# First-MLP weights of a two-layer encoder trunk: rounded by a casting DMA, with remainders formed by an adding DMA, in place of a plain load, a cast and a subtraction

## The chip, the cores and the metric

The kernel runs on one core of one Trainium2 chip. The metric is device time in microseconds: 1135.37 us as the median of 3 runs (1135.32 to 1135.9). An engine is named as the profile names it: PE (TensorE, matmuls), PEld (its weight loads), DVE (VectorE), ACT (ScalarE), POOL (GpSimd), SP (SyncE, whose queue issues all DMAs of the kernel before).

## The reference

The input x has 512 tokens of 1024 features. Two layers, each a token mixer and an MLP:

```python
for i in range(DEPTH):                      # DEPTH = 2: latent attention, then mLSTM
    hn = rms_norm(x, norm_mix[i])
    y = mla_mixer(hn, ...) if i == 0 else mlstm_mixer(hn, ...)
    x = x + y
    x = x + sqrelu_mlp(rms_norm(x, norm_ffn[i]), ffn_w1[i], ffn_w2[i])

def sqrelu_mlp(h, w1, w2):                  # w1: 1024 x 4096, w2: 4096 x 1024
    return jnp.square(jax.nn.relu(h @ w1)) @ w2
```

All in float32. The change touches the loading of w1 alone.

## The kernel before

**Products of three.** Every large product is made of operands that are split in two: `hi`, the value rounded to the short float type that PE takes (fp32r), and `lo`, the remainder, rounded likewise. `mm3` (L175) multiplies hi by hi, hi by lo and lo by hi into one accumulator. For weights the split is `split_w` (L155): the raw float32 tile `wr` arrives by DMA (`load_raw`, L150, on SP's queue), ACT casts it to `wh` (hi), DVE subtracts `wh` from `wr` and writes `wl` (lo). Each of the tags `wr`, `wh`, `wl` has three buffers that rotate.

**The stages.** `mla`, `ffn` of layer 0 (about 240 to 581 us), `mlstm`, `ffn` of layer 1 (about 810 to 1134 us). The MLP's hidden size of 4096 is worked in 8 chunks of 512, each as four blocks of 128 hidden features. A block ("F", `f_mm`, L749) is 24 matmuls: 8 slices of the model dimension, three products each, 512 tokens wide. Its third matmul is the first to read `wl`. After it, ACT applies relu and the square (`f_post`, L755); after every second block (odd numbers) POOL forms four sums over the squares (the tile `z`, four instructions in a row, 128x256 each), which ACT and DVE then split into `hh` and `hl`.

The second product uses a scheme with 7 products ("P", `s_mm`, L806) in place of 8 for each chunk but the last, each of 12 matmuls. Its weights come by SP as float32 tiles `tw` and are combined by POOL into t1, t2, t3, t4 (`s_sum`, L792, 128x1024 each) before they are split like the others.

**The order of the work.** It is written out: `units` (L867 to L874) lists blocks and products in PE's order. It begins with blocks 0 to 4; then, in a chunk, with the blocks named after their place:

```
P0 Fa P1 P2 Fb P3 P4 Fc P5 Fd P6
```

Fa of the first chunk is block 5, Fb block 6, and so on to block 28; the last chunk has only blocks 29, 30, 31, after its first, second and fourth product. When PE is at one unit, `ahead` (L877) loads the block that is four units further on (`f_load`, L743) and splits the weights of the unit that is two units further on (`f_split`, L746, or `s_split`, L803). Blocks 0 and 1 are loaded and split earlier, in `out_proj` (L712), and are not touched by the change, which leaves 30 blocks in each MLP.

Inside `ffn` all engines keep the order of the program for what is issued through `ipe`, `idve`, `iact` and `ipool` (L83, L731); so each engine works down one queue. `f_post` puts its four z sums on POOL's queue at once and the splits of z one and two units later (`later`, L783).

Of the kernel before, what the change touches and what calls it, by code (L numbers as in the profile page):

```python
# [16 lines left out]
F32 = mybir.dt.float32  # L17
F32R = mybir.dt.float32r
AF = mybir.ActivationFunctionType
# [3 lines left out]
P = 128  # L23
T = 512
NB = T // P
D = 1024
# [16 lines left out]
WMAX = 1280  # L43
# [18 lines left out]
def trunk(ctx: ExitStack, tc, a, yT, dbg=None):  # L62
    nc = tc.nc
    mult, add, sub, amax, amin, apow = ALU.mult, ALU.add, ALU.subtract, ALU.max, ALU.min, ALU.pow
    cp = ctx.enter_context(tc.tile_pool(name="cp", bufs=1))
    wp = ctx.enter_context(tc.tile_pool(name="wp", bufs=3))
# [16 lines left out]
    ipe, idve, iact, ipool = (InOrder(nc.tensor), InOrder(nc.vector), InOrder(nc.scalar, False), InOrder(nc.gpsimd, False))  # L83
    uid = [0]

    def nm(s):
        uid[0] += 1
        return f"{s}_{uid[0]}"
# [61 lines left out]
    def load_raw(src, n):  # L150
        raw = wp.tile([P, WMAX], F32, tag="wr", name=nm("wr"))
        nc.sync.dma_start(raw[:, :n], src)
        return raw

    def split_w(raw, n, act=nc.scalar, dve=nc.vector, dve2=None, m=0, to=None):  # L155
        if to is not None:
            hi, lo = to[0], to[1]
        else:
            hi = wp.tile([P, WMAX], F32R, tag="wh", name=nm("wh"))
            lo = wp.tile([P, WMAX], F32R, tag="wl", name=nm("wl"))  # L160
        if act in (nc.scalar, iact):
            act.copy(hi[:, :n], raw[:, :n])  # L162
        else:
            act.tensor_copy(hi[:, :n], raw[:, :n])
        if dve is dve2 or not dve2:
            dve.tensor_sub(lo[:, :n], raw[:, :n], hi[:, :n].bitcast(F32))  # L166
        else:
            dve.tensor_sub(lo[:, :m], raw[:, :m], hi[:, :m].bitcast(F32))
            dve2.tensor_sub(lo[:, m:n], raw[:, m:n], hi[:, m:n].bitcast(F32))
        return hi, lo  # L170
# [555 lines left out]
    def ffn(fp, layer, last):  # L726
# [12 lines left out]
        zs, hs, raws, ws, tw, bank, later, s_now = {}, {}, {}, {}, {}, {}, [], [1]  # L739
# [1 line left out]


        def f_load(i):  # L743
            raws[i] = load_raw(a["w1"][layer, i // 4 * 4 + (0, 2, 1, 3)[i % 4]], D)

        def f_split(i):  # L746
            ws["F", i] = split_w(raws.pop(i), D, iact, idve)

        def f_mm(ps, i, c=slice(0, T)):  # L749
            hi, lo = ws["F", i]  # L750
# [126 lines left out]
        def ahead(s_):  # L877

            if s_ + 4 < len(units) and units[s_ + 4][0] == "F":
                f_load(units[s_ + 4][1])  # L880
            if s_ + 2 < len(units):
                u = units[s_ + 2]
                if u[0] == "F":
                    f_split(u[1])
                else:
                    s_split(u[1], u[2])
                    if u[2] == 0:
                        s_sum(u[1], "t2")
                    elif u[2] == 1:
                        s_sum(u[1], "t4")  # L890


        ws["F", 0], ws["F", 1] = norm.first
        f_load(2)
        ps = [ps_mm(), ps_mm()]
        f_mm(ps[0], 0, HALVES[0])
        for do in norm.tail:
            do()
        f_mm(ps[1], 1, HALVES[0])
        f_load(3)  # L900
        f_split(2)
        f_mm(ps[0], 0, HALVES[1])
        f_post(ps[0], 0)
        f_mm(ps[1], 1, HALVES[1])
        f_load(4)
        f_split(3)
        f_post(ps[1], 1)
        s_load(0, ("b11", "b12"))
# [371 lines left out]
```

## Time and profile before

| | |
|---|---|
| median of 3 runs | 1135.37 us (1135.32 to 1135.9) |
| profiled execution, its own time | 1136.02 us |
| span of the profiled execution | 1134.0 us |
| granted TensorE clock, mean over the span | 0.998 of full speed |
| PE busy | 1111.6 us (98%) |
| DVE busy | 823.3 us (73%) |
| ACT busy | 557.9 us (49%) |
| POOL busy | 451.4 us (40%) |
| DMA | 104.27 MB, 30.1% of 16 engines' span, all on SP's queue but instructions |

How to read it. All times are from one profiled execution and count from its span's start; 2.0 us of its time lie around the span. A timeline's row gives the start, the duration, the engine, the line, the operation with output and inputs, how many instructions were merged (their time is then that of the row), and, in brackets, how long the engine idled before and whom it waited for. Matmuls overlap: on PE the distance between two starts (0.23 us for 512 columns) is what a matmul costs, and its duration is longer. Many instructions carry line 80, which is the helper that records them; they are told apart by their tiles. DMA-issuing instructions are not counted as busy.

### The profile page before, as it was taken

The numbers are of one execution on the slowest core, as the hardware profiler recorded it, in microseconds if no ns is written. First come the engines' busy times: TensorE is split into PE (matmuls) and PEld (weight loads), VectorE is DVE, ScalarE is ACT, GpSimd is POOL, SyncE is SP. The second block draws the span as 40 slices with busy tenths as digits, with TensorE's granted clock in tenths as the row PEclk, the third lists the DMA queues.
The fourth block names the chain that finished last, engine by engine and source line by source line (L and its number), as shares of the span: only waits on it lengthen the run. The fifth ranks groups of instructions, "written<-read, shape, count | busy, mean of one in ns | idle before, by whom it ended". The sixth has DMA issues, their size and how long they took to land.

```text
span 1134.0 us, 15668 instructions
## 1 busy us (share of the span) xinstructions
PE 1111.6 (98%) x5802; PEld 949.0 (84%) x5802; DVE 823.3 (73%) x1286; ACT 557.9 (49%) x985; POOL 451.4 (40%) x454
## 2 busy tenths in 40 slices
PE   7899999999999999999999999999999999999998
PEld 7889988888888888888898898888888888888886
DVE  7689997456798798788756565554578779779863
ACT  4468876336544444534545344332655444444441
POOL 6667785207356347335010011000537437436500
PEclk9999999999999999999999999999999999999999
DMA  6301021433432432343203223232343343333112
GB/s 202 117 25 47 20 76 38 132 98 124 128 99 74 127 112 84 102 123 89 85 21 100 87 59 91 81 90 86 136 113 91 93 130 93 93 112 111 57 56 75
DMA packets 32428, 104.27 MB, mean 92 GB/s; under 512 B 3424, under 2 KB 6752, under 8 KB 32352
## 3 DMA queue, kind: packets, MB, share of 16 engines
q1 hardware_dynamic: 32352, 103.27, 30.1%
q8 instruction: 46, 0.75, 0.3%
q14 instruction: 30, 0.25, 0.1%
HBM read 101.16 MB, written 2.10 MB: 91 GB/s over the span
## 4 chain that ended last, share of the span: by engine, by line
PE 93%; DVE 3%; POOL 2%; ACT 1%; issue 1%; DMA 0%; SPq 0%; ACTq 0%; POOLq 0%
PE mm L80 39%; PE tp L80 38%; PE mm L178 4%; PE mm L177 4%; PE mm L176 4%; PE po L80 3%; PE tp L178 1%; PE tp L177 1%; PE tp L176 1%; DVE wl L80 1%; ACT t L80 1%; DVE x L80 1%; POOL x L80 0%; DMA x<-in_xT 0%; POOL scr L80 0%
## 5 line engine op out<-in xcount | busy, mean ns | idle before, releaser
L80 PE MATMUL mm<-xg,wh 128*128 128x512 f32 (+1 forms) x1088 | 319.1, 377 | 0.0
L80 POOL TENSOR_TENSOR z<-z 128x256 f32<-128x256 f32 x112 | 129.5, 1175 | 320.2 <-ACT z L80 318.0
L80 PEld LDWEIGHTS mm<-xg,wh 128*128 128x128 f32 x1088 | 200.2, 188 | 37.4
L80 DVE TENSOR_TENSOR wl<-tw,wh 128x1024 fp32r<-128x1024 f32 x100 | 174.5, 1745 | 74.9 <-ACT wh L80 74.9
L80 PE MATMUL mm<-xg,wl 128*128 128x512 f32 (+1 forms) x544 | 206.3, 379 | 0.0
L80 POOL TENSOR_TENSOR tw<-tw,tw 128x1024 f32<-128x1024 f32 x56 | 159.8, 2862 | 34.6 <-issue 29.2
L80 DVE SCALAR_TENSOR_TENSOR x<-tp,r,x 128x512 f32<-128x512 f32 (+1 forms) x215 | 149.8, 733 | 14.2 <-PE tp L80 14.1
L80 PE MATMUL tp<-wh,hl 128*128 128x512 f32 x408 | 159.0, 390 | 0.9 <-DVE hl L80 0.9
L80 DVE TENSOR_TENSOR wl<-wr,wh 128x1024 fp32r<-128x1024 f32 (+1 forms) x72 | 119.6, 1661 | 55.4 <-ACT wh L80 55.4
L80 PE MATMUL tp<-wh,hh 128*128 128x512 f32 x408 | 159.1, 390 | 0.0
L80 PE MATMUL tp<-wl,hh 128*128 128x512 f32 x408 | 158.7, 389 | 0.0
L80 ACT ACTIVATE t<-mm 128x512 f32<-128x512 f32 (+3 forms) x97 | 54.3, 560 | 204.1 <-PE mm L80 195.0
L80 PEld LDWEIGHTS mm<-xg,wl 128*128 128x128 f32 x544 | 102.3, 188 | 22.9 <-DVE wl L80 4.5
L80 ACT CAST wh<-tw 128x1024 fp32r<-128x1024 f32 x100 | 104.7, 1047 | 34.1 <-PE tp L80 26.2
L80 ACT CAST wh<-wr 128x1024 fp32r<-128x1024 f32 (+1 forms) x74 | 78.9, 1067 | 32.1 <-PE tp L80 27.7
L166 DVE TENSOR_TENSOR wl<-wr,wh 128x1024 fp32r<-128x1024 f32 (+2 forms) x43 | 51.2, 1194 | 55.8 <-ACT wh L162 55.6
L80 PEld LDWEIGHTS tp<-wh,hl 128*128 128x128 f32 x408 | 76.6, 188 | 17.7 <-DVE hl L80 1.7
L80 PEld LDWEIGHTS tp<-wh,hh 128*128 128x128 f32 x408 | 76.6, 188 | 16.5 <-ACT zw L80 0.8
L80 PEld LDWEIGHTS tp<-wl,hh 128*128 128x128 f32 x408 | 76.6, 188 | 15.8
L80 ACT CAST hh<-z 128x1024 fp32r<-128x1024 f32 (+1 forms) x60 | 56.9, 949 | 53.0 <-POOL z L80 53.0
L80 DVE TENSOR_TENSOR hl<-z,hh 128x1024 fp32r<-128x1024 f32 (+1 forms) x60 | 80.7, 1345 | 0.0
L162 ACT CAST wh<-wr 128x1024 fp32r<-128x1024 f32 (+2 forms) x43 | 42.8, 995 | 66.7 <-PE mm L177 31.6
(281 smaller groups left out, 2063.7 us busy)
## 6 DMA issues: line engine op xcount, KB each, us to landing
wr<-in_w SPq DMA_DIRECT2D x64, 512.0 KB, 3.6
tw<-in_w SPq DMA_DIRECT2D x64, 512.0 KB, 3.6
wr<-in_w_qkv SPq DMA_DIRECT2D x8, 640.0 KB, 4.1
wr<-in_w_oa SPq DMA_DIRECT2D x8, 512.0 KB, 3.7
wr<-in_w_mo SPq DMA_DIRECT2D x8, 512.0 KB, 3.5
wr<-in_w_ob SPq DMA_DIRECT2D x8, 512.0 KB, 3.6
wr<-in_w_v SPq DMA_DIRECT2D x6, 512.0 KB, 3.9
wr<-in_w_z SPq DMA_DIRECT2D x8, 336.0 KB, 4.9
```

What stands on the lines that cost most here:

```text
L80: return lambda *args, **kw: tc.keep_in_program_order(f(*args, **kw)) if self.on else f(*args, **kw)
L162: act.copy(hi[:, :n], raw[:, :n])
L166: dve.tensor_sub(lo[:, :n], raw[:, :n], hi[:, :n].bitcast(F32))
L176: pe.matmul(out, lhsT=lh, rhs=rh, start=start, stop=False)
L177: pe.matmul(out, lhsT=lh, rhs=rl, start=False, stop=False)
L178: pe.matmul(out, lhsT=ll, rhs=rh, start=False, stop=stop)
```

## The change

`f_load` no longer loads float32 through SP. It takes a buffer of the tag `wr` as fp32r tile (`wfh`) and lets POOL issue a DMA from the float32 weights into it, which is to round on the way. `f_split` no longer casts on ACT and subtracts on DVE: ACT writes the negated rounded weights into `wl`, and a second DMA, issued by POOL, reads the same weights from HBM once more and adds them to `wl`. PE multiplies the same `hi` and `lo` in the same order. Blocks 0 and 1 of each MLP, and all other weights, stay as they were.

```diff
         def f_load(i):
-            raws[i] = load_raw(a["w1"][layer, i // 4 * 4 + (0, 2, 1, 3)[i % 4]], D)
+
+            raws[i] = wp.tile([P, WMAX], F32R, tag="wr", name=nm("wfh"))
+            ipool.dma_start(raws[i][:, :D], f_src(i))
+
+        def f_src(i):
+            return a["w1"][layer, i // 4 * 4 + (0, 2, 1, 3)[i % 4]]
 
         def f_split(i):
-            ws["F", i] = split_w(raws.pop(i), D, iact, idve)
+
+            hi = raws.pop(i)
+            lo = wp.tile([P, WMAX], F32R, tag="wl", name=nm("wl"))
+            iact.activation(lo[:, :D], hi[:, :D].bitcast(F32), AF.Copy, scale=-1.0)
+            ipool.dma_start(lo[:, :D], f_src(i), accum_op=add)
+            ws["F", i] = hi, lo
```

On POOL's queue, one chunk in the middle of the first MLP, from the z sums after a block Fc to the z sums after the next block Fa. `z` are the sums over squares, `tw` the weight sums t1, t2, t3, t4 in this order. Before:

```order
L80 TENSOR_TENSOR z_4153<-z_4153 128x256 x4
L80 TENSOR_TENSOR tw_4259<-tw_4122,tw_4120 128x1024
L80 TENSOR_TENSOR tw_4120<-tw_4197,tw_4259 128x1024
L80 TENSOR_TENSOR tw_4122<-tw_4197,tw_4122 128x1024
L80 TENSOR_TENSOR tw_4259<-tw_4195,tw_4120 128x1024
L80 TENSOR_TENSOR z_4293<-z_4293 128x256 x4
```

And now, with the DMAs behind the second z sums as well (`wfh` is a load, `wl` an adding DMA):

```order
L80 TENSOR_TENSOR z_4144<-z_4144 128x256 x4
L80 DMA wfh_4238<-in_w 128x1024
L80 TENSOR_TENSOR tw_4248<-tw_4113,tw_4111 128x1024
L80 TENSOR_TENSOR tw_4111<-tw_4187,tw_4248 128x1024
L80 DMA wl_4298<-in_w 128x1024
L80 TENSOR_TENSOR tw_4113<-tw_4187,tw_4113 128x1024
L80 DMA wfh_4318<-in_w 128x1024
L80 TENSOR_TENSOR tw_4248<-tw_4185,tw_4111 128x1024
L80 TENSOR_TENSOR z_4282<-z_4282 128x256 x4
L80 DMA wl_4379<-in_w 128x1024
L80 DMA wfh_4398<-in_w 128x1024
L80 DMA wfh_4457<-in_w 128x1024
```

The adding DMA of the next Fa (`wl_4298`) stands behind t1 and t2, that of Fb (`wl_4379`) behind the four z sums of Fa; the adding DMAs of Fc and Fd follow the two loads that end the piece.

On ACT's queue, the same place, from the relu of a block Fd to the split for P1. Before:

```order
L80 ACTIVATE t_4294<-mm_4261 128x512
L80 ACTIVATE z_4293<-t_4294 128x2x256
L80 CAST wh_4309<-wr_4249 128x1024
L80 CAST wh_4332<-tw_4259 128x1024
L80 CAST wh_4364<-tw_4120 128x1024
```

And now:

```order
L80 ACTIVATE t_4283<-mm_4250 128x512
L80 ACTIVATE z_4282<-t_4283 128x2x256
L80 ACTIVATE wl_4298<-wfh_4238 128x1024
L80 CAST wh_4320<-tw_4248 128x1024
L80 CAST wh_4352<-tw_4111 128x1024
```

The cast of the block's weights has become the negated copy, in the same place.

On POOL's queue, the start of the first MLP. Before:

```order
L80 TENSOR_TENSOR z_3529<-z_3529 128x256 x4
L80 TENSOR_TENSOR tw_3576<-tw_3574,tw_3572 128x1024
L80 TENSOR_TENSOR tw_3574<-tw_3580,tw_3574 128x1024
L80 TENSOR_TENSOR tw_3572<-tw_3580,tw_3576 128x1024
L80 TENSOR_TENSOR z_3616<-z_3616 128x256 x4
```

And now (`wfh_3411`, `wfh_3499`, `wfh_3556`, `wfh_3606` load blocks 2, 3, 4, 5; `wl_3501`, `wl_3558`, `wl_3608` add for blocks 2, 3, 4):

```order
L80 DMA wfh_3411<-in_w 128x1024
L80 DMA wfh_3499<-in_w 128x1024
L80 DMA wl_3501<-in_w 128x1024
L80 DMA wfh_3556<-in_w 128x1024
L80 DMA wl_3558<-in_w 128x1024
L80 TENSOR_TENSOR z_3528<-z_3528 128x256 x4
L80 TENSOR_TENSOR tw_3574<-tw_3572,tw_3570 128x1024
L80 TENSOR_TENSOR tw_3572<-tw_3578,tw_3572 128x1024
L80 DMA wfh_3606<-in_w 128x1024
L80 DMA wl_3608<-in_w 128x1024
L80 TENSOR_TENSOR tw_3570<-tw_3578,tw_3574 128x1024
L80 TENSOR_TENSOR z_3613<-z_3613 128x256 x4
```

The adding DMA of block 4 stands behind two weight sums and the load of block 5. PE's queue is the same in both kernels; DVE's has lost 60 subtractions, SP's 60 loads, and nothing else on them has moved.

## Rows read from the trace of the kernel before

**Rows 1.** The page: PE's busy time, and the chain that ended last by engine.

```profile
PE 1111.6 (98%) x5802; PEld 949.0 (84%) x5802; DVE 823.3 (73%) x1286; ACT 557.9 (49%) x985; POOL 451.4 (40%) x454
...
PE 93%; DVE 3%; POOL 2%; ACT 1%; issue 1%; DMA 0%; SPq 0%; ACTq 0%; POOLq 0%
```

**Rows 2.** PE's waits in the two MLPs: us in total, times, longest us.

```profile
PE tp L80 <- DVE hl L80: 0.4, 1, 0.4
PE mm L80 <- DVE xg L80: 0.3, 1, 0.3
...
PE mm L80 <- DVE x L80: 0.9, 1, 0.9
PE tp L80 <- DVE hl L80: 0.5, 1, 0.5
```

**Rows 3.** Timeline of PE, a chunk of the first MLP: beginnings of Fb, Fc, Fd, Fa.

```profile
370.59 0.62 PE L80 MATMUL mm<-xg,wh 128*128 128x512 f32 x2
371.04 0.39 PE L80 MATMUL mm<-xg,wl 128*128 128x512 f32 x1
...
381.92 0.39 PE L80 MATMUL mm<-xg,wl 128*128 128x512 f32 x1
...
390.08 0.39 PE L80 MATMUL mm<-xg,wl 128*128 128x512 f32 x1
...
400.51 0.61 PE L80 MATMUL mm<-xg,wh 128*128 128x512 f32 x2
```

**Rows 4.** Timeline of ACT, same chunk: casts for Fb, Fc, Fd and Fa.

```profile
366.52 1.03 ACT L80 CAST wh<-wr 128x1024 fp32r<-128x1024 f32 x1
...
377.39 1.03 ACT L80 CAST wh<-wr 128x1024 fp32r<-128x1024 f32 x1
...
381.67 1.05 ACT L80 CAST wh<-wr 128x1024 fp32r<-128x1024 f32 x1 [1.66 <-PE tp L80]
...
396.43 1.04 ACT L80 CAST wh<-wr 128x1024 fp32r<-128x1024 f32 x1
```

**Rows 5.** Groups by form, DVE, 240 to 581 us: busy, mean ns, idle before.

```profile
L80 DVE TENSOR_TENSOR wl<-wr,wh 128x1024 fp32r<-128x1024 f32 x31 | 54.6, 1760 | 27.5 <-ACT wh L80 27.5
L80 DVE TENSOR_TENSOR hl<-z,hh 128x768 fp32r<-128x768 f32 x14 | 20.9, 1491 | 0.0
```

**Rows 6.** The page's DMA issues: KB each, us from issue to landing.

```profile
wr<-in_w SPq DMA_DIRECT2D x64, 512.0 KB, 3.6
```

**Rows 7.** Timeline of SP's queue: one such load being issued.

```profile
401.05 0.33 SPq L152 DMA_DIRECT2D wr<-in_w  x1
```

**Rows 8.** Groups by form, whole span: POOL's instruction on 128x4 elements.

```profile
L80 POOL TENSOR_TENSOR scr<-sm,nhalf 128x4 f32<-128x4 f32 x32 | 34.0, 1064 | 2.4
```

**Rows 9.** Busy time by stretch (length, engines, granted clock, DMA share, GB/s).

```profile
8.00:9.00 1.00, 1.00 (x5) 0.98 (x6) 0.65 (x3) 0.58 (x1) 0.00 (x0) 1.00 1.09 393
```

**Rows 10.** Timeline of POOL, same chunk: z sums of Fa, then t1, then t2, t3.

```profile
366.69 4.83 POOL L80 TENSOR_TENSOR z<-z 128x256 f32<-128x256 f32 x4 [0.84 <-ACT z L80]
...
393.05 2.41 POOL L80 TENSOR_TENSOR tw<-tw,tw 128x1024 f32<-128x1024 f32 x1
396.68 6.60 POOL L80 TENSOR_TENSOR tw<-tw,tw 128x1024 f32<-128x1024 f32 x2 [1.22 <-issue]
```

**Rows 11.** Timeline of POOL, start of the first MLP: first two weight sums.

```profile
263.93 4.87 POOL L80 TENSOR_TENSOR tw<-tw,tw 128x1024 f32<-128x1024 f32 x2
```

**Rows 12.** Timeline of PE, start of the first MLP: block 4's third matmul.

```profile
269.13 0.39 PE L80 MATMUL mm<-xg,wl 128*128 128x512 f32 x1
```

**Rows 13.** Busy time by stretch in the attention stage, columns as in Rows 9.

```profile
62.00:64.00 2.00, 0.54 (x5) 0.30 (x3) 1.16 (x5) 1.17 (x4) 1.92 (x3) 1.00 0.00 0
64.00:66.00 2.00, 1.32 (x6) 0.97 (x7) 2.00 (x10) 0.25 (x1) 2.00 (x3) 0.96 0.19 34
66.00:68.00 2.00, 2.00 (x9) 1.81 (x9) 1.56 (x8) 0.57 (x2) 1.63 (x3) 0.50 0.79 289
68.00:70.00 2.00, 1.99 (x13) 1.75 (x11) 1.66 (x6) 1.05 (x5) 1.58 (x3) 0.68 0.03 13
```

## The prediction

> **What bounds the kernel now.** I read the page first, then TensorE's waits, then one chunk engine by engine in the timeline.
>
> [rows 1] PE is busy for 98% of the span and makes 93% of the chain that ended last; DVE makes 3%. [rows 2] In the two stages that the change touches (240 to 581 us, and 810 to 1134 us) PE waited 0.4, 0.3, 0.9 and 0.5 us, 2.1 us in all, each for a DVE result of another kind (hl, xg, x), none for a first-MLP remainder. So there is next to nothing to win there: what the change takes off DVE, PE doesn't wait for. What can move the time is a remainder (`wl`) that comes later than PE's third matmul of the block, the first one that reads it.
>
> How near that is shows in one chunk. [rows 3] Block Fb begins at 370.59 and reads its remainder at 371.04, 0.45 us later; Fc reads its at 381.92, Fd at 390.08; the next chunk's Fa begins at 400.51, so it reads at 400.96. [rows 4] ACT makes these four rounded copies at 366.52, 377.39, 381.67 and 396.43, and DVE has some 2 us left for the subtraction behind the first two.
>
> **The change, part by part.**
>
> *DVE.* 60 subtractions leave it: 30 blocks in each of the two MLPs. [rows 5] They cost 1.76 us each there, some 106 us in all. No wait of PE hangs on them [rows 2], so I put the gain at nothing.
>
> *ACT.* 60 casts become 60 scaled copies of the same tile in the same place of ACT's order. I price them as the casts, 1.03 to 1.05 us [rows 4], and the difference at nothing.
>
> *SP.* 60 loads leave its queue, which then holds only second-MLP loads. PE waits for none of these [rows 2]: nothing.
>
> *POOL.* 120 DMAs come in, and they stand in POOL's queue between its sums. The load of a block is issued four units before its use and can be late without harm. The adding DMA is the critical one: it can start only when ACT has the negated copy **and** POOL is past what stands ahead of it. Before, ACT and DVE alone made the remainder.
>
> Price of one adding DMA, D, from POOL being free to the tile having landed. No row shows a DMA issued by POOL or one that adds. [rows 6] A plain 512 KB load lands 3.6 us after its issue, of which [rows 7] 0.33 us is SP's own issuing. POOL's issuing: at least SP's 0.33; I take 1.06 us, POOL's instruction on 128x4 elements [rows 8], the nearest thing to a fixed cost there. The adding: at least nothing, at most a second transfer of 3.6 us; I take one more pass of 512 KB at the best rate that the trace has, 393 GB/s [rows 9], 1.33 us, since the tile must be read as well as the weights. D = 3.6 - 0.33 + 1.06 + 1.33 = 5.7 us. Ends: 3.6 (SP's price, nothing for adding) and 3.27 + 1.06 + 3.6 = 7.9. The Trainium skill (DMA: Bandwidth & Descriptors, Anatomy of one DMA) fits 2.0 us plus bytes over 436 GB/s to a DMA issued from POOL, an estimate of 3.2 us for 512 KB, against 3.6 from SP in the trace; by it (and a second pass at its 436 GB/s, 1.2) D would be 5.5 and the sum below some 8 us less.
>
> Now the four places, on the old clock of the chunk:
>
> - **A, block Fb.** Its adding DMA stands behind the four z sums [rows 10], which wait for ACT's squares of Fa. They end at 366.69 + 4.83 = 371.52; plus 5.7 is 377.2; PE reads at 371.04. Late by 6.2 us. Blocks 6, 10, ... 26: 6 times in each MLP.
> - **B, block Fc.** POOL is free, ACT's copy ends at 377.39 + 1.03 = 378.42; plus 5.7 is 384.1; PE reads at 381.92. Late by 2.2 us. Blocks 7, 11, ... 27 and 31: 7 times.
> - **C, the next Fa.** Its adding DMA stands behind the weight sums t1 and t2. [rows 10] t1 takes 2.41; t2 starts at 396.68 and takes 2.41, or 3.30 (half of 6.60) while DVE subtracts, as it did for the removed block; I take 2.41: 399.09, plus 5.7 is 404.8; PE reads at 400.96. Late by 3.8 us. Blocks 9, 13, ... 29: 6 times. The new load ahead of t1 falls into the 1.22 us that POOL idled there, and t3, t4 and the z sums behind it have time enough, since PE is late too.
> - **Fd** has a block more: 381.67 + 1.05 + 5.7 = 388.4, read at 390.08. Nothing.
> - **S, the start of the MLP**, block 4: [rows 11] two weight sums end at 263.93 + 4.87 = 268.80, then stands block 5's load (1.06), then this DMA: 275.6; [rows 12] PE reads at 269.13. Late by 6.4 us, once. Blocks 2 and 3 have their copies before POOL is busy; block 5 then comes just in time.
>
> Every late arrival counts in full: each chain starts from the end of a block on PE (ACT's squares, ACT's copy), so a delay of PE moves the next chain with it and is not made up. Per MLP 6 x 6.2 + 7 x 2.2 + 6 x 3.8 + 6.4 = 81.8 us; two of them 163.6 us.
>
> *The clock.* [rows 13] Before 66 us PE idled 2.1 of 4 us; the granted clock then stood at 0.50, which is 1.2 of 2.4 GHz, and came back before 70 us: in clock-microseconds 0.08 + 1.00 + 0.64 = 1.72 us were lost. A, C and S leave PE idle for longer than that. 13 per MLP, 26 in all, at 1.72 us: 44.7 us. B idles about 2 us beside full blocks; I count none there.
>
> Sum: 1136.0 (the profiled execution, whose median over the runs shown is 0.65 us lower) + 163.6 + 44.7 = 1344.3; against the median 1344.
>
> With D = 3.6 the places are late by 4.1, 0.1, 1.7 and 3.6 us: 78 us, and 1214; with clock drops at A and S alone 1238. With D = 7.9 and the long t2 they are 8.4, 4.4, 6.9 and 8.6: 262 us, with a clock drop at all 40 places 69 more: 1467.
>
> **Rivals.**
>
> *Not slower.* The mechanism: POOL hands its DMA out while its sums still run, so the DMA follows ACT's copy alone, and it lands soon. A has its copy at 366.52 + 1.03 = 367.55, 3.5 us ahead of PE's read, B 3.5 us, C 3.5 us: from D = 3.5 down nothing is late, and the time is 1134 to 1136. For it: POOL's sums wait where a DMA need not. Against it: the DMA stands behind them in one queue, and 3.5 is less than the plain load's 3.6 without any adding. 3%. The same with D = 5.7 would be late by 2.2 us at 19 places per MLP: 84 us, 1220; 4%.
>
> *The clock holds.* If PE's idling at A, C and S doesn't lower it, 1299. Against it stands the drop in [rows 13]. 10%.
>
> *Adding is far dearer than moving.* If the adding DMA went through its elements at a pace of its own, say D = 12, the places would be late by 12.5, 8.5, 10.1 and 12.7 us, 416 us in all, with the clock 1621. No row speaks for it; none excludes it. 5%.
>
> *POOL's DMAs wait for DVE.* An adding DMA that must first see DVE's instruction through pays up to 1.49 us, DVE's split of 128x768 [rows 5]: at 40 places 60 us, 1404. 4%. The Trainium skill (SBUF — State Buffer, two separate sides) has such a trap, in which DVE keeps POOL from writing the descriptors of its DMA; it names copies and casts for it and not the subtractions that DVE runs here, and no run here shows it.
>
> *The DMA doesn't round.* If it only moves the bits, the remainders are zeros, with the same instructions and waits: 1344 all the same.
>
> **How the numbers follow.** Chain and clock as above 74%; 1344 us. The rest as given. The range reaches from 1225, between the two readings of the lowest D, to 1470, above the highest; it leaves out the dear adding, the not slower case and most of the 1220 one. A measurement of this kernel tells 0.2%, about 2.3 us, from no change. Faster 0.02 and same 0.01 are the first rival; slower 0.97.
>
> **What would show it.** In the profile after: PE's waits in both MLPs name a DMA into wl; some 20 waits in each, of about 6, 2 and 4 us, three in a chunk that lengthens from 41 us to some 57 us; the adding DMA of Fb issued right behind the z sums; the clock at half behind the long waits; DVE's busy time down by some 100 us. I am wrong if PE waits for no DMA there, if Fb's adding DMA is issued before the z sums end, or if D is far from 5.7 us: each microsecond of D is some 40 us of time.

## The result, and the profile after

The changed kernel takes 1367.72 us (median of 4 runs, 1361.46 to 1371.88), the kernel before 1135.46 us in the same session (4 runs, 1135.32 to 1135.9): a ratio of 1.204, 95% interval [1.201, 1.207]. The forecast was 1344 us in 1225 to 1470, slower with a chance of 0.97.

The page of the kernel after, from its profiled execution of 1361.46 us: busy time; the two DMA queues (packets, MB, share of 16 engines); the chain by engine; two groups of instructions; DMA issues (KB, us to landing):

```profile
span 1359.7 us, 15679 instructions
...
PE 1177.4 (87%) x5802; PEld 988.3 (73%) x5802; DVE 725.0 (53%) x1226; ACT 555.9 (41%) x985; POOL 510.8 (38%) x574
...
q0 software_dynamic: 17280, 62.92, 21.1%
q1 hardware_dynamic: 23712, 71.81, 15.9%
...
PE 58%; DMA 17%; DVE 9%; ACT 7%; POOL 5%; issue 3%; SPq 0%; ACTq 0%; POOLq 0%; DVEq 0%
...
wfh<-in_w POOLq DMA_DIRECT2D x60, 512.0 KB, 5.3
wl<-in_w POOLq DMA_DIRECT2D x60, 512.0 KB, 5.4
```

Beside [rows 1]: PE makes 58% of the chain where it made 93%, and DMA, which made nothing, makes 17%. DVE lost 823.3 - 725.0 = 98 us of work, and nobody had waited for it. A second queue is there, `software_dynamic`, which is POOL's: 62.92 MB are 120 tiles of 512 KB. PE's own busy time rose by 66 us with the same 5802 matmuls: 61.2 us of that are a slower clock, below. The other 4.6 us, about 0.1 us for each of the 42 waits that follow, no row explains.

PE's waits in the kernel after (us in total, times, longest), which answer to [rows 2]:

```profile
PE mm L80 <- DMA wl<-in_w: 161.0, 42, 7.8
```

No other wait of PE grew. The span is 1359.7 - 1134.0 = 225.7 us longer: 161.0 us are this wait. For the clock I summed, over stretches of half a microsecond, PE's busy time by one minus the granted clock: 28.6 us in the first MLP (14 falls) and 32.5 in the second (14), 61.2 in all. The one fall of the kernel before, 1.7 us in the attention stage [rows 13], is in this kernel too, beside these. Together 222.2 of 225.7 us.

The three late places in one chunk of the first MLP, in the timeline of the kernel after (start, duration, engine, instruction, idle before it and releaser):

```profile
408.08 3.67 POOL L80 TENSOR_TENSOR z<-z 128x256 f32<-128x256 f32 x4 [6.88 <-ACT z L80]
411.70 0.86 POOL L80 DMA_DIRECT2D wl<-in_w  x1
...
417.12 0.79 PE L80 MATMUL mm<-xg,wl 128*128 128x512 f32 x1 [4.53 <-DMA wl<-in_w]
...
424.94 1.05 ACT L80 ACTIVATE wl<-wfh 128x1024 fp32r<-128x1024 f32 x1
...
426.29 0.89 POOL L80 DMA_DIRECT2D wl<-in_w  x1 [12.61 <-ACT wl L80]
...
431.81 0.50 PE L80 MATMUL mm<-xg,wl 128*128 128x512 f32 x1 [2.17 <-DMA wl<-in_w]
...
443.67 2.42 POOL L80 TENSOR_TENSOR tw<-tw,tw 128x1024 f32<-128x1024 f32 x1
...
447.10 1.21 DVE L80 TENSOR_TENSOR hl<-z,hh 128x1024 fp32r<-128x1024 f32 x1
...
447.31 3.28 POOL L80 TENSOR_TENSOR tw<-tw,tw 128x1024 f32<-128x1024 f32 x1 [1.23 <-PE tp L80]
450.52 0.87 POOL L80 DMA_DIRECT2D wl<-in_w  x1
...
455.98 0.80 PE L80 MATMUL mm<-xg,wl 128*128 128x512 f32 x1 [4.84 <-DMA wl<-in_w]
```

Read it in threes. Place A (block Fb): the z sums end at 411.7, the adding DMA is issued at once, and PE gets its tile at 417.12, 5.42 us later. Place B (Fc): ACT's negated copy ends at 425.99, the DMA goes out at 426.29, the tile is there at 431.81, 5.52 us later. Place C (the next Fa): t1 and t2 end at 450.5, issue at 450.52, tile at 455.98, 5.46 us later. One price, three things that it starts behind.

The clock behind A and B of that chunk, and behind another B (stretch, length, busy time of five engines, granted clock, DMA share, GB/s):

```profile
317.63 0.80 PE L80 MATMUL mm<-xg,wl 128*128 128x512 f32 x1 [2.23 <-DMA wl<-in_w]
...
318.00:320.00 2.00, 2.00 (x6) 1.52 (x6) 0.00 (x0) 0.00 (x0) 0.00 (x0) 0.50 0.91 158
...
415.00:417.00 2.00, 0.00 (x0) 0.00 (x0) 2.00 (x3) 0.00 (x0) 0.00 (x0) 0.91 1.01 256
417.00:419.00 2.00, 1.88 (x5) 1.49 (x5) 0.19 (x1) 0.00 (x0) 0.00 (x0) 0.50 1.09 395
419.00:421.00 2.00, 2.00 (x8) 1.65 (x7) 0.00 (x0) 0.00 (x0) 0.00 (x0) 0.74 1.04 408
...
432.00:434.00 2.00, 2.00 (x10) 1.62 (x10) 0.00 (x0) 0.00 (x0) 0.00 (x0) 1.00 0.89 158
```

After the 4.53 us wait the clock stands at 0.50, 1.2 of 2.4 GHz, where PE works again, and is at full speed again by 421. After a wait of 2.23 us it fell (318), after one of 2.17 us it didn't (432).

### The profile page after: what moved, and what is told of

Read it like the earlier page. It is cut to its first block, busy times and chain, and to the rows that moved or that the text cites. A ratio compares the mean times of both kernels' runs of the same rounds, so it can differ in the third digit from the quotient of the medians.

```text
span 1359.7 us, 15679 instructions
## 1 busy us (share of the span) xinstructions
PE 1177.4 (87%) x5802; PEld 988.3 (73%) x5802; DVE 725.0 (53%) x1226; ACT 555.9 (41%) x985; POOL 510.8 (38%) x574
## 3 DMA queue, kind: packets, MB, share of 16 engines
q0 software_dynamic: 17280, 62.92, 21.1%
q1 hardware_dynamic: 23712, 71.81, 15.9%
## 4 chain that ended last, share of the span: by engine, by line
PE 58%; DMA 17%; DVE 9%; ACT 7%; POOL 5%; issue 3%; SPq 0%; ACTq 0%; POOLq 0%; DVEq 0%
PE mm L80 31%; DMA wl<-in_w 17%; PE tp L80 14%; DVE wl L80 4%; PE mm L178 3%; PE mm L177 3%; PE mm L176 3%; POOL z L80 3%; DVE x L80 2%; PE po L80 2%; DVE hl L80 2%; ACT t L80 2%; ACT wh L80 2%; ACT z L80 1%; ACT wl L80 1%
## 5 line engine op out<-in xcount | busy, mean ns | idle before, releaser
L80 PE MATMUL mm<-xg,wl 128*128 128x512 f32 (+1 forms) x544 | 235.5, 433 | 161.0 <-DMA wl<-in_w 161.0
L80 PE MATMUL mm<-xg,wfh 128*128 128x512 f32 x960 | 334.9, 434 | 0.0
L80 PEld LDWEIGHTS mm<-xg,wl 128*128 128x128 f32 x544 | 116.8, 215 | 201.3 <-DMA wl<-in_w 178.7
L80 PEld LDWEIGHTS mm<-xg,wfh 128*128 128x128 f32 x960 | 208.3, 217 | 47.1
L80 POOL TENSOR_TENSOR z<-z 128x256 f32<-128x256 f32 x112 | 110.6, 1008 | 171.7 <-ACT z L80 169.5
L80 POOL TENSOR_TENSOR tw<-tw,tw 128x1024 f32<-128x1024 f32 x56 | 156.2, 2804 | 38.7 <-DVE wl L80 23.5
L80 POOL DMA_DIRECT2D wl<-in_w x60 | 53.3, 888 | 270.0 <-ACT wl L80 265.5
L80 PEld LDWEIGHTS tp<-wh,hh 128*128 128x128 f32 x408 | 76.6, 188 | 16.5 <-ACT zw L80 0.8
L80 ACT ACTIVATE wl<-wfh 128x1024 fp32r<-128x1024 f32 x60 | 63.3, 1055 | 47.7 <-PE tp L80 24.8
```

The lines of the kernel that those rows point to most:

```text
L80: return lambda *args, **kw: tc.keep_in_program_order(f(*args, **kw)) if self.on else f(*args, **kw)
```

## The experiments

My theory: the change costs what the late remainders cost, as PE's waits and as the clock's falls behind them. The wait has three terms: what the adding DMA is queued behind on POOL, a plain DMA's time, and the adding. Rivals: contention or slower matmuls beside the added traffic; a clock that falls for another reason; a cost that lies elsewhere on POOL. Times are medians of 4 runs where no other number is given; ratios are to the kernel before as it ran beside each experiment (1135.2 to 1135.5 us).

**1. Later need.** Each block's 16 matmuls on the rounded weights first, its 8 on the remainders last (cut from f_mm):

```diff
-                mm3(ps[:, c], hi[:, w], lo[:, w], xg[k][0][:, c], xg[k][1][:, c], k == 0, k == KD - 1, ipe)
+                ipe.matmul(ps[:, c], lhsT=hi[:, w], rhs=xg[k][0][:, c], start=k == 0, stop=False)
+                ipe.matmul(ps[:, c], lhsT=hi[:, w], rhs=xg[k][1][:, c], start=False, stop=False)
+            for k in range(KD):
+                w = slice(k * P, (k + 1) * P)
+                ipe.matmul(ps[:, c], lhsT=lo[:, w], rhs=xg[k][0][:, c], start=False, stop=k == KD - 1)
```

> The block's 24 matmuls in another order: the 16 that read the rounded weights first, the 8 that read the remainder last; nothing else changes. The remainder is then needed 16 x 0.227 = 3.63 us after the block's first matmul in place of 0.45, that is 3.2 us later. Theory (PE waits because the remainder lands late at fixed places): PE's waits fall from about 4.5 (behind the z sums), 2.1 (behind ACT's copy) and 4.85 us (behind t1 and t2) to about 1.3, 0 and 1.7, some 47 us in both MLPs instead of 161, the clock hardly drops, and the time is about 1190 us. Rival (the POOL DMAs and the second reading of the weights slow the stage as traffic, wherever the remainder is read): the time stays within 1330 to 1370 us.

Measured: 1194.65 us (1193.07 to 1195.48), ratio 1.0505 [1.0447, 1.0564], mean clock 0.990. PE's waits:

```profile
PE mm L80 <- DMA wl<-in_w: 44.2, 25, 4.6
```

Not one DMA, sum or byte differs from the changed kernel, and 173 of its 232 us are gone. The remainder is now first read 16 x 0.227 = 3.6 us into the block, in place of 0.45 us: B's waits vanish, A's shrink to 1.5 us or less, C's to 1.9 us or less except at block 29 (4.2 and 4.6 us). What is left is late remainders too: 44.2 us of waits and 9.2 us of clock, summed as above, are 53 of the 57 us that its span is over the kernel before. Lateness is the cost, not the added traffic.

**2. The z sums behind the adding DMA.** In f_post of the changed kernel:

```diff
-            ipool.tensor_add(z[:, S1], z[:, A21], z[:, A22])
...
+            def sums():
+                ipool.tensor_add(z[:, S1], z[:, A21], z[:, A22])
...
+            later.append([s_now[0] + 1, sums])
```

> Only the order on POOL's queue: the four z sums after an odd block are put one unit later, behind the adding DMA of the next-but-two unit's block. Theory (the queue position is a price of its own): only the places behind the z sums change, from 4.5 to about 2 us, since their DMA then follows ACT's copy alone; 12 x 2.5 = 30 us less waiting, and the 12 clock drops there (about 1.9 us each) mostly go; the other places stay: about 1315 us. Rival (the DMA's own duration is all, the queue position nothing): 1360 to 1370 us.

Measured: 1311.12 us (1303.48 to 1316.99), ratio 1.1523 [1.1454, 1.1593]. PE's waits:

```profile
PE mm L80 <- DMA wl<-in_w: 120.8, 41, 7.2
```

Place A goes from about 4.5 us to about 2 (2.96 and 2.80 us at the first A of each MLP), as long as B now. So the z sums in the queue ahead were a term of A, as the prediction said.

**3. The adding alone.** A plain DMA in place of the adding one, from the same place of the same queue. The remainders are left out: the tile holds rounded weights instead.

```diff
-            ipool.dma_start(lo[:, :D], f_src(i), accum_op=add)
+            ipool.dma_start(lo[:, :D], f_src(i))
```

> The second DMA of each block is a plain one: it writes the rounded weights into the remainder's tile over ACT's negated copy and adds nothing, so the remainders are left out and the rounded weights count twice. All queues and waits are the same. Theory (the price of one adding DMA is 5.4 us, of which the adding is 1.3 us or more): every wait of PE gets shorter by that much, to about 3, 0.7 and 3.4 us, about 95 us in both MLPs, and the time is about 1270 us. Rival (adding costs nothing over a plain DMA issued by POOL): the time stays at 1360 to 1370 us.

Measured: 1282.82 us (1275.02 to 1291.7), ratio 1.1281 [1.1204, 1.1357]. PE's waits, and the page's DMA issues:

```profile
PE mm L80 <- DMA wl<-in_w: 94.2, 40, 4.7
```

```profile
wl<-in_w POOLq DMA_DIRECT2D x60, 512.0 KB, 3.8
```

The adding is worth 5.4 - 3.8 = 1.6 us in each transfer, or (161.0 - 94.2) / 42 = 1.6 us in each wait. With a plain DMA, B is late by 0.4 us only in most chunks, but A and C by about 3: the difference is what they stand behind in the queue, and it is the larger part of their 4.5 and 4.8 us.

**4. The loads alone.** The kernel before, with its 60 loads issued by POOL as plain DMAs, the rest as it was:

```diff
-            raws[i] = load_raw(a["w1"][layer, i // 4 * 4 + (0, 2, 1, 3)[i % 4]], D)
+            raws[i] = wp.tile([P, WMAX], F32, tag="wr", name=nm("wr"))
+            ipool.dma_start(raws[i][:, :D], a["w1"][layer, i // 4 * 4 + (0, 2, 1, 3)[i % 4]])
```

> The kernel before, with the 60 loads of first-MLP blocks issued by POOL in the place where the change issues its loads, but as plain float32 loads; cast and subtraction stay on ACT and DVE. Theory (a load on POOL's queue is early enough anywhere and costs nothing): 1135 to 1138 us, no wait of PE for it. Rival (POOL's issuing, between its sums, delays sums or loads so that PE waits): 1145 us or more, with waits of PE for a DMA into wr or for z.

Measured: 1144.04 us (10 runs, 1142.84 to 1144.99), ratio 1.0068 [1.0048, 1.0088]. My theory missed: a load on POOL is not free here. Its waits of PE, and the timeline around one:

```profile
PE mm L80 <- DVE wl L80: 6.5, 12, 0.6
```

```profile
393.89 1.45 POOL L80 TENSOR_TENSOR z<-z 128x256 f32<-128x256 f32 x1
395.29 0.57 POOL L80 DMA_DIRECT2D wr<-in_w  x1
...
399.21 1.06 ACT L80 CAST wh<-wr 128x1024 fp32r<-128x1024 f32 x1 [0.43 <-DMA wr<-in_w]
...
403.91 0.50 PE L80 MATMUL mm<-xg,wl 128*128 128x512 f32 x1 [0.54 <-DVE wl L80]
```

The load stands behind the z sums until 395.29 and lands 3.9 us later; ACT waits for it, DVE's subtraction after it ends too late, and PE waits 0.54 us, 12 times, at C. The weight loads in front of these matmuls show more of it: they wait 11.6 us there, and 4.5 in the kernel before (experiment 8). `hl` at the start of each MLP is late by 1.28 and 1.16 us, where it was by 0.4 and 0.5 [rows 2]. The rival's line of 1145 us is not quite reached, but its mechanism is what shows. In the changed kernel the late load at C is covered, since t2 lets the adding DMA go later still (450.52, when the copy has been there since 448.69).

**5. The clock alone.** The changed kernel with 608 matmuls of no use put where PE waits:

```diff
+            if i > 3 and i not in (5, 8, 12, 16, 20, 24, 28, 30):
+                d = pp.tile([P, 512], F32, tag="po", bufs=1, name=nm("po"))
+                for _ in range((20, 20, 18, 8)[i % 4]):
+                    ipe.matmul(d, lhsT=hi[:, 0:P], rhs=xg[0][0], start=True, stop=True)
```

> The changed kernel, with 8 to 20 matmuls of no use (into a spare PSUM tile) put ahead of each block whose remainders come late, about as long as PE's wait there (18 x 0.227 = 4.1 us ahead of the blocks behind the z sums, 20 = 4.5 us ahead of those behind t1 and t2, 8 = 1.8 us ahead of those behind ACT's copy); nothing is left out. Theory (the waits are set by the adding DMAs, and PE's idleness in them is what lowers the granted clock afterwards): the blocks start no later than before, the waits of PE for wl shrink to under 40 us in all since the added matmuls stand in them, and the lowered clock goes almost wholly: mean clock over 0.99, 1367.7 - 61 = about 1307 us (1295 to 1320). Rival (the clock falls for another cause, such as the DMAs or the power drawn, or the added matmuls only lengthen PE's work): clock still about 0.94 and 1365 us or more.

Measured: 1307.57 us (1303.6 to 1311.1), ratio 1.1518 [1.1492, 1.1545]. Its cores and its waits of PE:

```profile
core 0: 1309.3 us, clock 0.992
```

```profile
PE mm L80 <- DMA wl<-in_w: 23.7, 31, 3.6
```

608 x 0.227 = 138 us of work took the place of 137.3 us of waiting, so the blocks begin about as late as ever, and the kernel is 60 us faster by doing more. Four falls are left in the MLPs, 6.8 us of clock, each behind one of the four waits that stayed over 2 us. That settles the clock's share, about 60 of the 232 us, and, since every DMA is the same, its cause: PE's idling.

**6. Both queue terms.** Experiment 2, and t2 behind the adding DMA where a block of the first product follows (cut from `ahead`):

```diff
                     f_split(u[1])
+                    if ("F", u[1]) in due:
+                        s_sum(due.pop(("F", u[1])), "t2")
...
-                        s_sum(u[1], "t2")
+                        if units[s_ + 3][0] == "F":
+                            due[units[s_ + 3]] = u[1]
+                        else:
+                            s_sum(u[1], "t2")
```

> The kernel in which the four z sums stand behind the block's adding DMA (1311 us, waits for wl 120.8 us), and with t2 put behind the adding DMA too where a block of the first product comes next; nothing is left out. Theory (what the adding DMA is queued behind on POOL is a term of its own, beside the transfer's own 5.4 us from ACT's copy): the waits behind t1 and t2 go from 4.1 to about 2 us, 12 x 2.1 = 25 us less, so some 95 us of waits for wl, fewer falls of the clock (10 to 40 us), 1225 to 1270 us, about 1250. Rival (the blocks behind t1 and t2 are late because the DMA itself is slow there, beside the other transfers): the waits there stay at 4 us and the time at about 1311 us.

Measured: 1265.94 us (1257.31 to 1269.82), ratio 1.1136 [1.1085, 1.1186]. PE's waits:

```profile
PE mm L80 <- DMA wl<-in_w: 88.5, 41, 3.6
```

Nearly every block now waits the same, 1.8 to 2.4 us in the timeline of the first MLP: what is left is the DMA's own time behind ACT's copy.

**7. Experiments 6 and 1 together.**

> Both: z sums and t2 behind the adding DMA, and each block's 16 matmuls on the rounded weights ahead of its 8 on the remainders; nothing is left out. Theory (lateness of the remainders is all that the change costs): waits of 2 us vanish under the 3.6 us that the 16 matmuls give; what is left are the first blocks of each MLP and block 29 (about 3 + 4 us in each MLP), so 1134 + 14 + a few us of clock and of the loads on POOL: 1140 to 1160 us. Rival (the change has a price apart from lateness, such as contention in SBUF or PE slowed beside the adding transfers): over 1175 us.

Measured: 1164.31 us (1161.76 to 1168.54), ratio 1.0261 [1.0233, 1.0289], above what I expected. PE's waits:

```profile
PE mm L80 <- DMA wl<-in_w: 15.9, 18, 2.0
PE tp L80 <- DVE hl L80: 6.6, 2, 3.6
```

The first row is near the 14 us foreseen by luck alone. I had expected four waits of 3 to 4 us, in the first blocks and at block 29; there are none at those, but 18 of up to 2.0 us in the middle of the MLPs, at blocks of A and B, so the waits of 2 us did not all vanish. The second row is new: at the start of each MLP the deferred z sums make `hl` late by 3.0 and 3.6 us. A sum that is moved behind a DMA is late itself.

**8. A control.** The kernel before in the matmul order of experiment 1, the same edit.

> The kernel before with the order of matmuls of the first experiment alone (each block's 16 matmuls on the rounded weights first, then its 8 on the remainders); nothing is left out. A control of the reordering: by every theory 1135 us within 2 us. Over 1140 us the reordering has a price (or, under 1133, a gain) of its own that has to come off the readings of the other runs with it.

Measured: 1132.53 us (9 runs, 1131.16 to 1132.78), ratio 0.9975 [0.9966, 0.9985]: faster than the kernel before by 2.7 us, which I had not expected. That much is the reordering's own, and comes off the readings of experiments 1, 7 and 10. The waits of PE's weight loads in the kernel before, one of them in its timeline, and the attention stage in the control's stretches:

```profile
PEld mm L80 <- DVE wl L80: 4.5, 12, 0.4
```

```profile
401.07 0.19 PEld L80 LDWEIGHTS mm<-xg,wl 128*128 128x128 f32 x1 [0.38 <-DVE wl L80]
```

```profile
60.00:75.00 15.00, 12.03 (x88) 10.63 (x87) 12.56 (x48) 10.31 (x26) 13.09 (x21) 1.00 0.12 45
```

The kernel before did wait for first-MLP remainders: 12 times 0.38 us at C, in the weight load, where the view of PE's own waits shows nothing. The row of 4.5 us is gone in the control, and the second product's matmuls in each MLP cover 296.3 us from first to last start in place of 298.0 and 297.9. The fall of the clock of [rows 13], 1.7 us, is absent too. But it comes and goes between executions of one kernel: of the 12 runs of the kernel before beside this one, seven show a mean clock of 1.000. Their median is 1135.1 us, that of the control's three such runs 1132.5, so the gain is not the clock's.

**9. One place earlier.** The changed kernel, with copy and adding DMA three places of the order ahead in place of two, the loads five:

```diff
-            lo = wp.tile([P, WMAX], F32R, tag="wl", name=nm("wl"))
+            lo = wp.tile([P, WMAX], F32R, tag="wh" if i % 2 else "wl", name=nm("wl"))
...
-            if s_ + 4 < len(units) and units[s_ + 4][0] == "F":
-                f_load(units[s_ + 4][1])
+            for u in units[:s_ + 6]:
+                if u[0] == "F" and u[1] >= nxt[0]:
+                    f_load(u[1])
+                    nxt[0] = u[1] + 1
+            for u in units[:s_ + 4]:
+                if u[0] == "F" and u[1] >= nxt[1]:
+                    f_split(u[1])
+                    nxt[1] = u[1] + 1
...
```

> The changed kernel, with copy and adding DMA of every first-product block one place of the order earlier (three ahead of use, not two), and its load one place earlier too; the remainders of odd blocks take tiles of the ring of the rounded weights, since the ring of remainders has no fourth tile. All work is kept. A place of the order is 5.4 us, the transfer lands 5.4 us after POOL is free and PE waited 2.2 to 4.9 us. Theory (lateness is the whole cost): the waits behind the z sums, ACT's copy and t2 vanish, the first blocks of each MLP (4.9 and 7.0 us, not moved) and a fall of the clock behind each stay, so 1134 + 12 + 3 to 8 = 1145 to 1160 us. Rival (the adding transfers cost PE something apart from lateness: slower matmuls beside them, other weights' transfers held up, tiles not free in time): over 1175 us.

Measured: 1179.9 us (1167.6 to 1181.13), ratio 1.037 [1.0318, 1.0422]. PE's waits, and one of ACT's:

```profile
PE mm L80 <- DMA wl<-in_w: 19.6, 10, 6.5
PE tp L80 <- ACT wh L80: 7.0, 7, 1.3
PE tp L80 <- DVE wl L80: 6.1, 8, 0.8
...
ACT wl L80 <- DMA wfh<-in_w: 118.2, 27, 6.0
```

Over the rival's line of 1175, but by lateness again: PE's waits named and 9.4 us of clock make 42 of the 45 us that its span is over the kernel before. The first row fell from 161.0, and most of what is left of it is in the blocks at either end of an MLP (4.9, 2.4, 6.5, 2.6). The next two rows are a new lateness, of the second product's weights: ACT stands at the copies whose load has not landed (last row, 27 times), and the casts of those weights stand behind the copies, as the next experiment's timeline shows.

**10. The same with the order of experiment 1.**

> The same, with each block's 16 matmuls on the rounded weights ahead of its 8 on the remainders. All work is kept. Theory: only the first blocks of each MLP are late, by what the 16 matmuls (3.6 us) don't cover, some 1 to 4 us in each MLP and a fall of the clock behind it: 1132.5 (the kernel before in this order) + 4 to 10 = 1136 to 1143 us, not below 1132, since PE is the bound and the change takes no work from PE. Rival (the change gives something back once nothing is late, by DVE's 60 subtractions that are gone): under 1131 us; other rival as in the run before (a price apart from lateness): over 1150 us.

Measured: 1158.15 us (1152.44 to 1163.31), ratio 1.0205 [1.0162, 1.0249]: over the line of 1150, again with a new wait. Its timeline:

```profile
293.76 1.14 POOL L80 DMA_DIRECT2D wfh<-in_w  x2
...
299.16 1.06 ACT L80 ACTIVATE wl<-wfh 128x1024 fp32r<-128x1024 f32 x1 [4.27 <-DMA wfh<-in_w]
300.13 1.03 ACT L80 CAST wh<-tw 128x1024 fp32r<-128x1024 f32 x1
...
301.21 0.49 PE L80 MATMUL tp<-wh,hh 128*128 128x512 f32 x1 [1.14 <-ACT wh L80]
```

The load goes out behind the z sums at 293.76. ACT stands at the copy that needs it until 299.16, and the cast of a second-product weight stands behind that copy. Moved earlier, the adding DMA is in time, and its predecessor, the load on the same queue, is late next. PE's waits for `wl` (5.6 us) and for the second product's weights (7.1 and 4.6 us), with 5.1 us of clock, make 22.4 of the 24.7 us that its span is over the control's. No run of mine made the change free: 10 loses most of its time to waits that it made itself, and 7, the other near one, still 15.9 us to late remainders and 6.6 us to a wait of its own.

## Why the prediction was right, point by point

- **What bounds it.** Right that PE was the bound and that taking 98 us from DVE wins nothing. Not quite right that nothing waited for a remainder: 12 x 0.38 us did (experiment 8).
- **The price D.** 5.7 us forecast, 5.4 to 5.5 measured at A, B and C, and more where a load is issued right ahead of it: 7.6 us at block 4 (issued 267.56, load 266.98, PE gets the tile at 275.20), 7.9 at block 29, below. Its parts: the adding 1.6 us (1.33 taken), POOL's issue 0.86 to 0.89 (1.06 taken), the plain DMA from POOL 3.8 to landing. The Trainium skill (DMA: Bandwidth & Descriptors, Anatomy of one DMA) gave an estimate of 3.2 us for the latter; both runs with plain DMAs on POOL are above it (3.8, and 3.9 in experiment 4).
- **The places, first MLP.** A: 26.9 us forecast 37.2. The four z sums took 3.67 us in place of 4.83 [rows 10], because DVE no longer subtracts beside them: in experiment 9, where another weight's subtraction stands there (397.51, beside sums from 396.62), they took 4.65. I had taken the old duration. B: 15.3, forecast 15.4. C: 31.9, forecast 22.8. I took t2 as 2.41 us, arguing that the removed subtraction had made it 3.30; it stayed 3.28. That was a misreading of DVE's rows of the kernel before, below: the split of `hl` had already begun when t2 did at 396.68, as it has in the changed kernel (447.10, t2 at 447.31), while the removed subtraction began later and was itself the long one. Of the two durations that I had, the other was right. At block 29 it is 7.8, not 3.8, for another reason: its adding DMA is issued right behind the load of block 30 (621.10 after 620.52), so it takes 7.9 us. The start: 6.0 over blocks 2 to 4 (0.86, 0.25 and 4.89), forecast 6.4 at block 4 alone. Sum 80.1, forecast 81.8; both MLPs 161.0, forecast 163.6. That the sum came out so near is luck: errors of -10 at A and +9 at C cancelled.

```profile
396.46 1.21 DVE L80 TENSOR_TENSOR hl<-z,hh 128x1024 fp32r<-128x1024 f32 x1
397.60 3.42 DVE L80 TENSOR_TENSOR wl<-wr,wh 128x1024 fp32r<-128x1024 f32 x1
```

- **The clock.** 28 falls (26 forecast): all at A, C and block 4 as forecast, and two at B, where I had counted none (317.63, and block 31 of the second MLP). They cost 2.19 us each, not 1.72: 61.2 against 44.7. This term was mis-sized and makes most of the miss. The one fall that the trace before showed was of the short kind; in the changed kernel 12 of the 28 cost 1.4 to 1.7 us, and 16 cost 2.2 to 3.1, standing at half for about 7 us or more rather than 3.5.
- **The loads on POOL** "can be late without harm": true only because something else is later. Experiment 4 shows their own price, 8.5 us.
- **The sum.** 1367.7 - 1344 = 24 us: 16.5 of the clock, -2.6 of the waits, 3.5 left unexplained (the 4.6 us of PE's busy time above, less 1.1 us of other idling), and 6.3 by which the median lies over the profiled run. The profiled run's granted clock, 0.939, is the highest of the four (the others have 0.930 to 0.932), so that part points to the clock too. The rivals fell: the DMA did stand behind the sums, the clock did fall, adding is no 12 us, and no extra wait for DVE shows in D.

## What to carry to other kernels

Before moving work to a DMA, list what that DMA will stand behind in its queue and which instruction needs it first; the work taken off an engine that nobody waited for counts nothing beside that. A wait of PE of some microseconds can be paid again in the clock, here 61 us on top of 161, so ask for the lateness of each block rather than for a sum of busy times. Where an operand may be late, read it last in its group: the order of matmuls alone took 173 of 232 us back here, and 2.7 us from the kernel before, where the wait stood in the weight loads and not among PE's waits.

## What the runs showed of the hardware

An adding DMA costs more than a plain one. While one adding DMA ran alone, the 16 engines were almost full at 145 GB/s, each tile's 512 KB counted once; one of experiment 3's plain DMAs from POOL, alone as well, ran at 260 GB/s:

```profile
428.00:430.00 2.00, 1.63 (x8) 1.01 (x6) 1.79 (x3) 1.01 (x1) 0.00 (x0) 1.00 0.98 145
...
357.20:359.20 2.00, 2.00 (x10) 1.41 (x8) 1.82 (x3) 0.54 (x1) 0.00 (x0) 1.00 0.90 260
```

The Trainium skill (Collectives: The Full Stack, Stop ④ — SDMA + CCE: where bytes move and the add happens) counts a step that adds as read-read-write, with the add free in between. Here the adding transfer cost 1.6 us more for each 512 KB than the plain one; whether that is the second read or the addition, no run here separates.

POOL's 128x1024 subtraction took 2.4 us, but 3.3 us where DVE's split of `hl` had begun just before it (396.46 before, 447.10 after, 404.63 in experiment 9). DVE's subtraction of the same size, begun during one of POOL's, took 3.42 us (397.60) where it took 1.23 us at 367.58.

The granted clock's falls differ in length, and nearly the same wait may bring one or not (2.23 and 2.17 us, above). The time of a kernel that waits often spreads by some 10 us between runs (1361.46 to 1371.88 us here). The kernel before stays within 1134.2 to 1136.2 us in all of its 36 runs but one, which took 1146.54 us at a granted clock of 0.930.
